# A hybrid trunk layer: low weight parts kept in DRAM for a second use, low slices issued last, pools waiting by bytes

## The chip, the cores and the metric

The kernel runs on one core of one Trainium2 chip. A core has five engines that run their own instruction streams: TensorE (PE, matmuls, with its weight loads shown as PEld), VectorE (DVE), ScalarE (ACT), GpSimd (POOL) and SyncE (SP, which here only issues DMAs). The metric is the time of one execution on the device in microseconds (us). A profile is one such execution, recorded instruction by instruction.

## What is computed

One layer of a streaming encoder trunk on 1024 prompt tokens and 32 sample tokens, width 1024, all in fp32. Three mixers share one input projection, a merge and a layer norm follow, and then PEER, a layer of single-neuron experts: 8 heads, each choosing 16 of 128 x 128 experts by product keys.

```python
z = x @ w_in + b_in                      # 12 sections of 1024 columns
y_a = (a_b * conv3(a_c * a_x)) @ w_out_a
y_b = (gelu(b_g) * rg_lru(conv4(b_x) + conv_b_b)) @ w_out_b
y_c = (rmsnorm(hgrn2(silu(c_q), 1 - f, c_i, log(f))) * silu(c_g)) @ w_out_c
merged = sigmoid(g_a) * y_a + sigmoid(g_b) * y_b + sigmoid(g_c) * y_c
x = layer_norm(ALPHA * x + merged @ w_o)
x = layer_norm(ALPHA * x + peer(x))

def peer_block(xt, wq, keys, u_tab, v_tab):
    q = (xt @ wq).reshape(n, 8, 2, 128)
    s = einsum('nhpd,hpkd->nhpk', q, keys)
    sv, si = top_k(s, 16)                       # per half
    top_s, top_p = top_k(sv[:, :, 0, :, None] + sv[:, :, 1, None, :], 16)
    expert = cid[top_p]                         # si0 * 128 + si1
    g = softmax(top_s)
    h = gelu(einsum('nd,nhkd->nhk', xt, u_tab[expert]))
    return einsum('nhk,nhkd->nd', g * h, v_tab[expert])
```

## The kernel before

**Tiling.** Activations lie transposed, 128 channels by tokens. Tokens are worked in two blocks: b=0 with 512 prompt tokens, b=1 with the other 512, a gap of 3 and the 32 sample tokens (548 columns, cut in two pieces of 274). Projections work on weight tiles of 128 input channels x 8 slices x 128 output channels (512 KB).

**Projections in split precision.** `weight` (L286) makes one weight tile ready: SP loads the raw fp32 tile into `wraw` (L300), ACT rounds it to the high part `wh` (L292), DVE subtracts, which leaves the low part `wl` (L293). All three have two buffers in the pool `wp` (topk1 keeps eight in `wk`). Activations are split the same way into `h`/`l` pairs (`dh`/`dl` in the dense stage). `proj` (L319) runs over the 8 slices and issues for each, and for each piece of tokens, wh by high (L326) and wh by low (L327), and then wl by high (L329), all into one PSUM tile `z`.

**Stages.** `first` works block 0: the heads of mixer C with mixer A between them, the three output projections, `norm1` (w_o), and then the two halves of its top-k (topk0.0, topk0.1, 256 tokens each, weights wq), between which mixer A of block 1 is put. `last` works block 1: heads with output A and gates, outputs C and B, norm1 in two parts, topk1 in two parts. The layer's experts come by two ways:

- For block 0 `gather` fetches them: for each of four tiles of 128 tokens, 128 rows-per-token of u and 128 of v, each an indirect DMA of 512 KB issued by POOL (L1210) into one of four `row` buffers. DVE multiplies and sums a u row (L1219, with a read of the accumulator) and multiplies and adds a v row (L1227). These 1024 DMAs and 1024 DVE instructions run beside everything else from the end of topk0.0 on; how many stand beside each stage is given by the seven numbers of `BESIDE`, counted against PE's instructions between marks (`cuts`).
- For block 1 the dense stage computes all 16,384 experts. 40 hidden tiles are made ahead, one-hot weights are spread to DRAM (`gd`, L1072/1073), and then 16 times: 8 projections of `ut`, 8 of `vt` over 544 tokens, accumulated by DVE into `acc` (L1141).

**Which weights are used more than once.** w_in's 96 tiles twice (block 0 and 1), w_out_b's and w_out_c's 8 twice, w_o's 8 three times, wq's 16 in topk0.0, again in topk0.1, and 24 times in topk1. w_out_a goes in plain fp32 in block 1 (`proj32`). `ut` and `vt` (256 tiles) are used once.

**What orders the work.** A scheduler that simulates the program puts the instructions of every engine in an order when the kernel is built; each engine then runs its own in that order, and waits on semaphores. SP's DMAs are issued in order too, so one that waits holds those behind it. Pools of tiles are opened and closed by stage (`open`, L117); a pool opened over bytes of a closed one waits for the closed one to be done with.

The changed functions and what calls them:

Of the kernel before, what the change touches and what calls it, by code (L numbers as in the profile page):

```python
# [10 lines left out]
F32 = mybir.dt.float32  # L11
# [11 lines left out]
KT = 8  # L23
# [54 lines left out]
class Lay:  # L78


    def __init__(self, n, cut=None, o=0):
        self.N, self.o = n, o
        cut = cut or (n if n <= 512 else n // 2)
        self.segs = [(o, cut)] + ([(o + cut, n - cut)] if cut < n else [])
# [17 lines left out]
class K:  # L102
    def __init__(self, ctx, tc, io):
        self.ctx, self.tc, self.nc, self.io = ctx, tc, tc.nc, io
        pool = lambda name, bufs, **k: ctx.enter_context(tc.tile_pool(name=name, bufs=bufs, **k))
        self.cst = pool("cst", 1)
        self.xp = pool("xp", 8)
        self.wp = pool("wp", 2)
        self.bp = pool("bp", 1)
        self.gp = pool("gp", 1)  # L110
        self.dp = pool("dp", 1, space=bass.MemoryType.DRAM)
        self.wpool, self.nraw = (self.wp, 2), 0
        self.rawp = [self.wpool]
        self.fetched = {}
        self.xs, self.ms = ([], []), ([None] * 8, [None] * 8)
        self.consts()

    def open(self, ctx, **pools):

        for name, (bufs, kw) in pools.items():  # L120
            setattr(self, name, ctx.enter_context(self.tc.tile_pool(name=name, bufs=bufs, **kw)))

    def et(self, n=556, dt=F32):
        return self.ep.tile([128, n], dt, name="e", tag="e")
# [158 lines left out]
        V.memset(self.st, 0.0)  # L283


    def weight(self, ap):  # L286
        nc = self.nc
        raw = self.weight32(ap)
        pool, bufs = self.wpool
        wh = pool.tile([128, KT, 128], F32R, name="wh", tag="wh", bufs=bufs)  # L290
        wl = pool.tile([128, KT, 128], F32R, name="wl", tag="wl", bufs=bufs)
        nc.scalar.copy(wh, raw)  # L292
        nc.vector.tensor_sub(wl, raw, wh.bitcast(F32))  # L293
        return wh, wl

    def weight32(self, ap):
# [4 lines left out]
        return raw  # L301

    def win(self, sec, ct):
        return self.fetched.pop((sec, ct), None) or self.weight(self.io["w_in"][sec * 8 + ct])

    def split(self, t, n, pool):
        nc = self.nc
# [11 lines left out]
    def proj(self, w, x, lay):  # L319
        mm = self.nc.tensor.matmul  # L320
        z = self.zz(lay)
        wh, wl = w
        for k in range(KT):
            xh, xl = x[k]
            for (o, n), ps in zip(lay.segs, z):
                mm(ps[:, :n], wh[:, k, :], xh[:, o:o + n], start=k == 0, stop=False)  # L326
                mm(ps[:, :n], wh[:, k, :], xl[:, o:o + n], start=False, stop=False)  # L327
            for (o, n), ps in zip(lay.segs, z):
                mm(ps[:, :n], wl[:, k, :], xh[:, o:o + n], start=False, stop=k == KT - 1)  # L329
        return z  # L330
# [6 lines left out]
                                      start=k == 0, stop=k == KT - 1)  # L337
        return z

    def outp(self, ap, y, lay):  # L340
        if isinstance(y[0], tuple):
            return self.proj(self.weight(ap), y, lay)
        return self.proj32(self.weight32(ap), y, lay)

    def at(self, b):
# [46 lines left out]
    def first(self, pick):  # L392

        nc, b = self.nc, 0
        with ExitStack() as c:
            self.open(c, yq=(8, {}))
            self.ypool = None, self.yp
            self.at(0)
            self.fetched = {(C_F, 0): self.win(C_F, 0)}
            self.load(0)  # L400
            MARK(nc, "mix_ca0")
            y = []
            oraw = self.heads(lambda h: y.append(self.mix_a(h)))
            cm = c.enter_context(ExitStack())
            self.open(cm, mp=(8, {}))
            MARK(nc, "out_a0")
            for d in range(8):
                self.out_piece(d, "w_out_a", G_A, y)
                if d == RMS:
                    rs = self.rms(oraw)  # L410
            y, gs = self.outs(oraw, rs)
            MARK(nc, "out_b0")
            for d in range(8):
                self.join(d, "w_out_b", y, gs[d], L0)
            self.load(1)
            m = [self.yfin(t) for t in self.m]
            cm.close()
            with ExitStack() as c2:
                self.open(c2, np_=(2, {}))
                MARK(nc, "norm0")  # L420
                lng = self.lnvec("ln1_g", self.np_, 1), self.lnvec("ln1_b", self.np_, 1)
                xT = self.norm1(m, self.tiles(0), L0, lng, lambda: self.pair(self.yq, "yh", "yl"))
            self.open(c, rp=(12, {}))
            self.ypool = self.yp, None
            self.at(0)
            ya = []
            for i, part in enumerate((Lay(256), Lay(256, o=256))):
                self.at(1)
                MARK(nc, f"mix_a1.{i}")
                ya.append(self.mix_a(len(ya)))  # L430
                self.at(0)
                MARK(nc, f"topk0.{i}")
                unit, end = self.topk(self.tiles(0)[2 * i:2 * i + 2], part, xT)
                for hg in range(4):
                    unit(hg, lambda j: self.weight(self.io["wq"][hg * 4 + j]), self.keys(hg, self.ep))
                for f in end():
                    self.at(1)
                    pick(f)
                    if not self.cuts:
                        self.cuts.append(len(nc.cur_bb.bb.instructions))  # L440
                    ya.append(self.mix_a(len(ya)))
            return ya

    def last(self, ya, cy, cs):
        nc = self.nc
# [5 lines left out]
        with ExitStack() as c:  # L451
# [21 lines left out]
            y, _ = self.outs(oraw, self.rms(oraw), zg)  # L473
# [3 lines left out]
            with ExitStack() as c2:  # L477
# [8 lines left out]
                y = [self.halves(t, self.et(dt=F32R), over(self.y2, "y") if k else self.et(dt=F32R))  # L486
                     for k, t in enumerate(y)]
                m = []
# [9 lines left out]
        with ExitStack() as c:  # L498
            self.open(c, wk=(1, {}))
            MARK(nc, "topk1")  # L500
            parts = [self.topk(of(flat), flat, xT) for _, flat in PARTS]
            held = {}
            for i, hg in ORDER:
                if hg not in held:
                    keys = self.keys(hg, self.wk)
                    self.wpool = (self.wk, 8) if hg > 1 else (self.wp, 2)
                    f = lambda j, hg=hg: self.weight(self.io["wq"][hg * 4 + j])
                    ws = []
                    if hg > 1:
                        held[hg] = lambda j, ws=ws, f=f: ws[j] if j < len(ws) else ws.append(f(j)) or ws[j], keys  # L510
                parts[i][0](hg, *held.get(hg, (f, keys)))
            self.wpool = self.wp, 2
            return xT, [s for _, end in parts for s in end()]
# [322 lines left out]

    def join(self, d, wname, y, g, L):
        nc, V = self.nc, self.nc.vector
        py = self.outp(self.io[wname][d], y, L)
        new = self.m[d] is None  # L840
        m = self.m[d] = self.mp.tile([128, NG], F32, name="m", tag="m") if new else self.m[d]
        for v, p in L.each(py):
            V.scalar_tensor_tensor(v(m if new else g), v(g), 1.0, p, op0=OP.add, op1=OP.mult)
        if not new:
            c = slice(L.o, L.o + L.N)
            V.tensor_add(m[:, c], m[:, c], g[:, c])
# [28 lines left out]
    def norm1(self, m, tiles, lay, lng, x1):  # L875
        nc = self.nc
# [1 line left out]
        rT = []  # L878
        w = 556 // N
        for d in range(8):  # L880
            ps = self.outp(self.io["w_o"][d], m, lay)
            if d % w == 0:
                t = self.et()
            rT.append(t[:, d % w * N:(d % w + 1) * N])
            A.copy(rT[d], ps[0][:, :N])
        xT = [x1() for _ in range(KT)]
        for ti, g0, o, n in tiles:
# [11 lines left out]
            for half in range(2):  # L899
                pt = self.tt()  # L900
                for j in range(4):
                    k = half * 4 + j
                    nc.tensor.transpose(pt[:, j * 128:j * 128 + n], xt[:n, k * 128:(k + 1) * 128],
                                        self.ident[:n, :n])
                for j in range(4):
                    xh, xl = xT[half * 4 + j]
# [488 lines left out]
```

## Time and profile before

| | us |
| --- | --- |
| runs (3) | 4188.08, 4206.25, 4211.31 |
| median | 4206.25 |
| the profiled execution | 4205.61 |
| its span in the profile | 4203.8 |
| mean granted TensorE clock | 0.952 |
| PE busy | 3815.1 |
| DVE busy | 3389.8 |
| POOL busy | 1591.6 |
| ACT busy | 1461.2 |
| moved by DMA | 973.51 MB, mean 232 GB/s |

Busy times are those of instructions of one profiled execution. A group's row in the profile names line, engine, operation, the tile written and those read with their shapes, then the count, the busy time in us, the mean of one in ns, the idle time just before them and what ended most of it. A row of the waits gives the waiting engine, tile and line, what it waited for, then us in total, times, and the longest. The granted clock is a share of full speed.

### The profile page before, as it was taken

The page shows a single profiled execution, that of the slowest core. Times are in us where ns is not written, and L with a number is a line of the kernel's source. Part 1 is how long each engine was busy: PE and PEld are TensorE (multiplying, and loading weights), DVE is VectorE, ACT ScalarE, POOL GpSimd, SP SyncE. Part 2 cuts the span into 40 slices and gives each one's busy share as a digit, 9 for nine tenths or more (in the row PEclk, how much of TensorE's full clock was granted, in tenths as well). Part 3 has the DMA queues.
Part 4 walks back from the last instruction along what each step waited for, and adds up shares of the span by engine and source line. Part 5 has one row for each costly group of instructions (what it writes and reads, how often), then busy time and mean ns, then how long its engine had stood idle before and what let it go on. Part 6 is the DMA issues. An engine that isn't in the chain of part 4 may idle for free.

```text
span 4203.8 us, 69644 instructions
## 1 busy us (share of the span) xinstructions
PE 3815.1 (91%) x26917; PEld 3564.2 (85%) x26917; DVE 3389.8 (81%) x6793; ACT 1461.2 (35%) x2358; POOL 1591.6 (38%) x1353
## 2 busy tenths in 40 slices
PE   9999999998866998998878999789999999999997
PEld 7888777787765896998868999689999999999997
DVE  6565448589997787998899999967788878777888
ACT  3333337332212222454233389822222222222222
POOL 0000000002453344444552478823355555455553
PEclk9999999999887998999989999899999999999998
DMA  3222222345785666778986888698889988888886
GB/s 109 76 71 78 90 92 92 129 154 195 255 284 183 197 226 194 249 271 279 316 287 206 266 247 245 202 325 302 283 315 325 324 303 312 299 313 302 311 313 243
DMA packets 333451, 973.51 MB, mean 232 GB/s; under 512 B 29952, under 2 KB 104832, under 8 KB 331072
## 3 DMA queue, kind: packets, MB, share of 16 engines
q0 software_dynamic: 147456, 536.94, 37.6%
q1 hardware_dynamic: 185664, 432.12, 30.3%
q8 instruction: 212, 3.47, 0.3%
q14 instruction: 119, 0.97, 0.1%
HBM read 912.40 MB, written 56.54 MB: 230 GB/s over the span
## 4 chain that ended last, share of the span: by engine, by line
PE 50%; DVE 15%; issue 14%; DMA 10%; POOL 9%; ACT 2%; POOLq 0%; SPq 0%; DVEq 0%; ACTq 0%
PE z L329 14%; PE z L326 14%; PE z L327 14%; POOL row L1210 9%; DMA row<-in_v,ex 6%; DVE row L1219 2%; DVE wl L293 2%; DVE x1g L1227 2%; DMA row<-in_u,ex 2%; PE t L1073 2%; PE t L681 1%; PE z L336 1%; DVE oa L1069 1%; DVE e L960 1%; DVE e L959 1%
## 5 line engine op out<-in xcount | busy, mean ns | idle before, releaser
L326 PE MATMUL z<-h,wh 128*128 128x272 f32 (+5 forms) x4608 | 1381.8, 313 | 104.6 <-ACT xe L637 59.8
L327 PE MATMUL z<-l,wh 128*128 128x272 f32 (+5 forms) x4608 | 1377.5, 311 | 6.0 <-DVE l L908 4.8
L292 ACT CAST wh<-wraw 128x1024 fp32r<-128x1024 f32 x568 | 595.5, 1049 | 1850.5 <-PE z L327 1538.4
L1210 POOL DMA_INDIRECT row<-in_u,ex x512 | 669.0, 1307 | 1432.6 <-DVE ex L1033 667.5
L329 PE MATMUL z<-h,wl 128*128 128x272 f32 (+5 forms) x4608 | 1172.7, 312 | 10.2 <-DVE wl L293 10.1
L326 PEld LDWEIGHTS z<-h,wh 128*128 128x128 f32 x4608 | 883.0, 192 | 152.0 <-ACT xe L637 60.1
L1210 POOL DMA_INDIRECT row<-in_v,ex x512 | 682.9, 1334 | 797.5 <-DVE x1g L1227 532.2
L327 PEld LDWEIGHTS z<-l,wh 128*128 128x128 f32 x4608 | 883.4, 192 | 42.3 <-DVE l L908 5.9
L293 DVE TENSOR_TENSOR wl<-wraw,wh 128x1024 fp32r<-128x1024 f32 x568 | 692.4, 1220 | 232.5 <-ACT wh L292 231.2
L329 PEld LDWEIGHTS z<-h,wl 128*128 128x128 f32 x4608 | 778.3, 191 | 50.0 <-DVE wl L293 14.0
L1227 DVE SCALAR_TENSOR_TENSOR x1g<-row,hh,x1g 128x1024 f32<-128x1024 f32 x512 | 655.3, 1280 | 105.1 <-DMA row<-in_v,ex 101.6
L1219 DVE SCALAR_TENSOR_TENSOR row<-row,x1g 128x1024 f32<-128x1024 f32 x512 | 619.3, 1221 | 98.8 <-DMA row<-in_u,ex 98.0
L326 PE MATMUL z<-dh,wh 128*128 128x272 f32 x2048 | 556.2, 293 | 9.3 <-ACT ge L1084 4.9
L327 PE MATMUL z<-dl,wh 128*128 128x272 f32 x2048 | 558.2, 294 | 1.1 <-DVE dl L1128 1.1
L329 PE MATMUL z<-dh,wl 128*128 128x272 f32 x2048 | 436.0, 295 | 74.6 <-DVE wl L293 74.4
L326 PEld LDWEIGHTS z<-dh,wh 128*128 128x128 f32 x2048 | 391.5, 194 | 12.3 <-ACT ge L1084 5.2
L329 PEld LDWEIGHTS z<-dh,wl 128*128 128x128 f32 x2048 | 331.2, 194 | 79.4 <-DVE wl L293 79.4
L327 PEld LDWEIGHTS z<-dl,wh 128*128 128x128 f32 x2048 | 391.7, 193 | 1.7 <-DVE dl L1128 1.5
L1072 POOL TENSOR_SCALAR ob<-iota,tr 128x128 f32<-128x128 f32 x272 | 218.6, 818 | 29.4 <-PE t L1073 13.0
L329 PE MATMUL z<-yh,wl 128*128 128x512 f32 (+1 forms) x512 | 179.4, 353 | 22.5 <-DVE wl L293 22.4
L1127 ACT CAST dh<-w 128x544 fp32r<-128x544 f32 x128 | 82.5, 648 | 335.8 <-DVE w L1123 335.4
L1073 PE MATMUL t<-ob,oa 128*128 128x128 f32 x1088 | 172.8, 295 | 25.1 <-DVE oa L1069 8.5
(382 smaller groups left out, 4828.3 us busy)
## 6 DMA issues: line engine op xcount, KB each, us to landing
wraw<-in_w_in SPq DMA_DIRECT2D x192, 512.0 KB, 3.5
wraw<-in_vt SPq DMA_DIRECT2D x128, 512.0 KB, 6.4
wraw<-in_ut SPq DMA_DIRECT2D x128, 512.0 KB, 5.6
gd<-stg SPq DMA_DIRECT2D x34, 1024.0 KB, 6.1
gt<-gd SPq DMA_DIRECT2D x16, 2176.0 KB, 10.7
wraw<-in_wq SPq DMA_DIRECT2D x56, 512.0 KB, 4.3
wraw<-in_w_o SPq DMA_DIRECT2D x24, 512.0 KB, 4.9
hd<-ge SPq DMA_DIRECT2D x40, 272.0 KB, 4.8
```

The lines of the kernel that those rows point to most:

```text
L292: nc.scalar.copy(wh, raw)
L293: nc.vector.tensor_sub(wl, raw, wh.bitcast(F32))
L326: mm(ps[:, :n], wh[:, k, :], xh[:, o:o + n], start=k == 0, stop=False)
L327: mm(ps[:, :n], wh[:, k, :], xl[:, o:o + n], start=False, stop=False)
L329: mm(ps[:, :n], wl[:, k, :], xh[:, o:o + n], start=False, stop=k == KT - 1)
L336: self.nc.tensor.matmul(ps[:, :n], w[:, k, :], x[k][:, o:o + n], start=k == 0, stop=k == KT - 1)
L1072: G.tensor_scalar(ob, self.iota, tr[:, 1, t:t + 1], None, op0=OP.is_equal)
L1073: nc.tensor.matmul(pw[:, s * 128:(s + 1) * 128], oa, ob, start=True, stop=True)
L1127: A.copy(hi, w)
L1210: nc.gpsimd.indirect_dma_start(out=u[:n], out_offset=None, in_=self.io[tab], in_offset=bass.IndirectOffsetOnAxis(ap=ex[:n, s:s + 1], axis=0))
L1219: V.scalar_tensor_tensor(u[:n], u[:n], 1.0, x1[:n], op0=OP.mult, op1=OP.mult, accum_out=hh[:n, s:s + 1])
L1227: V.scalar_tensor_tensor(x1[:n], u[:n], hh[:n, s:s + 1], x1[:n], op0=OP.mult, op1=OP.add)
```

## The change

1. `weight` takes a key. At a key's first use the low part is computed as before and is also stored to a DRAM tile of its own (SP, new L301). At later uses SP loads it from there into `wl` (new L295), and DVE does no subtraction. Keys are given for w_in, w_out_b, w_out_c, w_o and wq: 136 stores and 168 loads of 512 KB.
2. `proj` issues all slices' high-weight matmuls first, and then all slices' low-weight matmuls (new L339).
3. `open` asks for pools that wait for the tiles whose bytes they take over, instead of for the whole closed pool.
4. `outp` takes the weight's name and index, which makes the key.

Line numbers move: the cast L292 to L293, the subtraction L293 to L297, raw loads L300 to L308, matmuls L326, L327, L329 to L334, L335, L339, the rows' DVE instructions L1219 and L1227 to L1230 and L1238, `ex` L1033 to L1044.

```diff
--- before.py
+++ after.py
@@ -111,14 +111,15 @@
         self.dp = pool("dp", 1, space=bass.MemoryType.DRAM)
         self.wpool, self.nraw = (self.wp, 2), 0
         self.rawp = [self.wpool]
-        self.fetched = {}
+        self.fetched, self.low = {}, {}
         self.xs, self.ms = ([], []), ([None] * 8, [None] * 8)
         self.consts()
 
     def open(self, ctx, **pools):
 
         for name, (bufs, kw) in pools.items():
-            setattr(self, name, ctx.enter_context(self.tc.tile_pool(name=name, bufs=bufs, **kw)))
+            setattr(self, name, ctx.enter_context(self.tc.tile_pool(
+                name=name, bufs=bufs, reuse_waits="tile", **kw)))
 
     def et(self, n=556, dt=F32):
         return self.ep.tile([128, n], dt, name="e", tag="e")
@@ -283,14 +284,21 @@
         V.memset(self.st, 0.0)
 
 
-    def weight(self, ap):
+    def weight(self, ap, key=None):
         nc = self.nc
         raw = self.weight32(ap)
         pool, bufs = self.wpool
         wh = pool.tile([128, KT, 128], F32R, name="wh", tag="wh", bufs=bufs)
         wl = pool.tile([128, KT, 128], F32R, name="wl", tag="wl", bufs=bufs)
         nc.scalar.copy(wh, raw)
+        if key in self.low:
+            nc.sync.dma_start(wl.bitcast(F32), self.low[key])
+            return wh, wl
         nc.vector.tensor_sub(wl, raw, wh.bitcast(F32))
+        if key:
+
+            self.low[key] = self.dp.tile([128, KT, 128], F32, name="wl%d" % len(self.low))
+            nc.sync.dma_start(self.low[key], wl.bitcast(F32))
         return wh, wl
 
     def weight32(self, ap):
@@ -301,7 +309,7 @@
         return raw
 
     def win(self, sec, ct):
-        return self.fetched.pop((sec, ct), None) or self.weight(self.io["w_in"][sec * 8 + ct])
+        return self.fetched.pop((sec, ct), None) or self.weight(self.io["w_in"][sec * 8 + ct], ("w_in", sec * 8 + ct))
 
     def split(self, t, n, pool):
         nc = self.nc
@@ -325,6 +333,8 @@
             for (o, n), ps in zip(lay.segs, z):
                 mm(ps[:, :n], wh[:, k, :], xh[:, o:o + n], start=k == 0, stop=False)
                 mm(ps[:, :n], wh[:, k, :], xl[:, o:o + n], start=False, stop=False)
+        for k in range(KT):
+            xh, _ = x[k]
             for (o, n), ps in zip(lay.segs, z):
                 mm(ps[:, :n], wl[:, k, :], xh[:, o:o + n], start=False, stop=k == KT - 1)
         return z
@@ -337,9 +347,10 @@
                                       start=k == 0, stop=k == KT - 1)
         return z
 
-    def outp(self, ap, y, lay):
+    def outp(self, name, d, y, lay):
+        ap = self.io[name][d]
         if isinstance(y[0], tuple):
-            return self.proj(self.weight(ap), y, lay)
+            return self.proj(self.weight(ap, name != "w_out_a" and (name, d)), y, lay)
         return self.proj32(self.weight32(ap), y, lay)
 
     def at(self, b):
@@ -432,7 +443,7 @@
                 MARK(nc, f"topk0.{i}")
                 unit, end = self.topk(self.tiles(0)[2 * i:2 * i + 2], part, xT)
                 for hg in range(4):
-                    unit(hg, lambda j: self.weight(self.io["wq"][hg * 4 + j]), self.keys(hg, self.ep))
+                    unit(hg, lambda j: self.weight(self.io["wq"][hg * 4 + j], ("wq", hg * 4 + j)), self.keys(hg, self.ep))
                 for f in end():
                     self.at(1)
                     pick(f)
@@ -504,7 +515,7 @@
                 if hg not in held:
                     keys = self.keys(hg, self.wk)
                     self.wpool = (self.wk, 8) if hg > 1 else (self.wp, 2)
-                    f = lambda j, hg=hg: self.weight(self.io["wq"][hg * 4 + j])
+                    f = lambda j, hg=hg: self.weight(self.io["wq"][hg * 4 + j], ("wq", hg * 4 + j))
                     ws = []
                     if hg > 1:
                         held[hg] = lambda j, ws=ws, f=f: ws[j] if j < len(ws) else ws.append(f(j)) or ws[j], keys
@@ -836,7 +847,7 @@
 
     def join(self, d, wname, y, g, L):
         nc, V = self.nc, self.nc.vector
-        py = self.outp(self.io[wname][d], y, L)
+        py = self.outp(wname, d, y, L)
         new = self.m[d] is None
         m = self.m[d] = self.mp.tile([128, NG], F32, name="m", tag="m") if new else self.m[d]
         for v, p in L.each(py):
@@ -878,7 +889,7 @@
         rT = []
         w = 556 // N
         for d in range(8):
-            ps = self.outp(self.io["w_o"][d], m, lay)
+            ps = self.outp("w_o", d, m, lay)
             if d % w == 0:
                 t = self.et()
             rT.append(t[:, d % w * N:(d % w + 1) * N])
```

The orders below list an engine's instructions with the numbers that the build gives to tiles; `wl0` to `wl135` are the new DRAM tiles.

SP near the start of the kernel, before, in the first use of w_in:

```order
L300 DMA wraw_361<-in_w_in 128x1024
L517 DMA keys_6744<-in_keys 128x512
L300 DMA wraw_394<-in_w_in 128x1024
L300 DMA wraw_427<-in_w_in 128x1024
L300 DMA wraw_464<-in_w_in 128x1024
```

and now:

```order
L308 DMA wraw_363<-in_w_in 128x1024
L528 DMA keys_6984<-in_keys 128x512
L301 DMA wl0_276<-wl_273 128x1024
L308 DMA wraw_398<-in_w_in 128x1024
L301 DMA wl1_369<-wl_366 128x1024
L308 DMA wraw_433<-in_w_in 128x1024
```

A store now stands between each two raw loads. SP at the start of block 1's heads, in the second use, before:

```order
L300 DMA wraw_10047<-in_w_in 128x1024
L300 DMA wraw_10107<-in_w_in 128x1024
L300 DMA wraw_10167<-in_w_in 128x1024
L300 DMA wraw_10231<-in_w_in 128x1024
L300 DMA wraw_10291<-in_w_in 128x1024
```

and now:

```order
L308 DMA wraw_10379<-in_w_in 128x1024
L295 DMA wl_10187<-wl47_3211 128x1024
L308 DMA wraw_10439<-in_w_in 128x1024
L295 DMA wl_10258<-wl0_276 128x1024
L308 DMA wraw_10503<-in_w_in 128x1024
L295 DMA wl_10322<-wl1_369 128x1024
```

Each low load follows the raw load of the weight two further on. DVE at the end of topk0, where block 0's last expert indices `ex` are made, before:

```order
L1219 SCALAR_TENSOR_TENSOR row_39394,hh_39061<-row_39394,x1g_39062 128x1024
L1027 TENSOR_REDUCE r_9364<-r_9398 128x8x8
L1017 TENSOR_TENSOR r_9378<-r_9377 128x128
L1024 TENSOR_TENSOR r_9402<-r_9378,io16_87 128x512
L1024 TENSOR_TENSOR r_9406<-r_9378,io16_87 128x1024
L1026 TENSOR_TENSOR r_9402<-r_9402,r_9312 128x512
L1026 TENSOR_TENSOR r_9406<-r_9406,r_9312 128x1024
L1027 TENSOR_REDUCE r_9364<-r_9402 128x8x8
L1027 TENSOR_REDUCE r_9364<-r_9406 128x8x8
L1033 SCALAR_TENSOR_TENSOR ex_9410<-r_9364 128x128
```

and now:

```order
L1230 SCALAR_TENSOR_TENSOR row_39531,hh_39333<-row_39531,x1g_39334 128x1024
L1035 TENSOR_TENSOR r_9674<-r_9650,io16_87 128x512
L1035 TENSOR_TENSOR r_9678<-r_9650,io16_87 128x1024
L1037 TENSOR_TENSOR r_9674<-r_9674,r_9584 128x512
L1230 SCALAR_TENSOR_TENSOR row_39534,hh_39333<-row_39534,x1g_39334 128x1024
L1037 TENSOR_TENSOR r_9678<-r_9678,r_9584 128x1024
L1038 TENSOR_REDUCE r_9636<-r_9674 128x8x8
L1230 SCALAR_TENSOR_TENSOR row_39537,hh_39333<-row_39537,x1g_39334 128x1024
L1038 TENSOR_REDUCE r_9636<-r_9678 128x8x8
L1230 SCALAR_TENSOR_TENSOR row_39540,hh_39333<-row_39540,x1g_39334 128x1024
L1044 SCALAR_TENSOR_TENSOR ex_9682<-r_9636 128x128
```

Row tiles are numbered in threes from row_39064 before and row_39336 now, so row_39394 was the 111th row and row_39540 is the 69th: fewer rows stand ahead of `ex`, more behind it. PE at the start of the dense stage, before:

```order
L326 MATMUL z_25466<-dh_25400,wh_25462 128x272
L327 MATMUL z_25466<-dl_25401,wh_25462 128x272
L326 MATMUL z_25467<-dh_25400,wh_25462 128x272
L327 MATMUL z_25467<-dl_25401,wh_25462 128x272
L329 MATMUL z_25466<-dh_25400,wl_25463 128x272
L329 MATMUL z_25467<-dh_25400,wl_25463 128x272
```

and now, around the border between the high and the low slices of that projection:

```order
L335 MATMUL z_25796<-dl_25721,wh_25792 128x272
L335 MATMUL z_25797<-dl_25721,wh_25792 128x272
L334 MATMUL z_25796<-dh_25728,wh_25792 128x272
L334 MATMUL z_25797<-dh_25728,wh_25792 128x272
L335 MATMUL z_25738<-dl_25729,wh_25734 128x272
L335 MATMUL z_25739<-dl_25729,wh_25734 128x272
L339 MATMUL z_25738<-dh_25672,wl_25735 128x272
L339 MATMUL z_25739<-dh_25672,wl_25735 128x272
```

The first matmul on the low part moves from the fifth of a projection's 48 matmuls to the 33rd, and here the scheduler has put high slices of the next projection (`z_25796`, `wh_25792`) ahead of it as well.

## The prediction

> **What bounds the kernel now.** I read the page's totals and groups, then a table of stretches between VectorE (DVE) landmarks (first top-k MAX8, last expert-index `ex`, last `sb` step, last scan, last residual split of norm1, last top-k of block 1, first `acc` add), then waits, chain and DMA of each stretch. The stretches' rows give length, then busy time with count for PE, its weight loads, DVE, ACT and POOL, the granted clock, DMA share and GB/s.
>
> ```profile
> span 4203.8 us, 69644 instructions
> PE 3815.1 (91%) x26917; PEld 3564.2 (85%) x26917; DVE 3389.8 (81%) x6793; ACT 1461.2 (35%) x2358; POOL 1591.6 (38%) x1353
> L293 DVE TENSOR_TENSOR wl<-wraw,wh 128x1024 fp32r<-128x1024 f32 x568 | 692.4, 1220 | 232.5 <-ACT wh L292 231.2
> L1227 DVE SCALAR_TENSOR_TENSOR x1g<-row,hh,x1g 128x1024 f32<-128x1024 f32 x512 | 655.3, 1280 | 105.1 <-DMA row<-in_v,ex 101.6
> L1219 DVE SCALAR_TENSOR_TENSOR row<-row,x1g 128x1024 f32<-128x1024 f32 x512 | 619.3, 1221 | 98.8 <-DMA row<-in_u,ex 98.0
> ...
> core 0: us, PE busy (x) PEld busy (x) DVE busy (x) ACT busy (x) POOL busy (x), PEclk, DMA share, GB/s
> 0.00:896.00 896.00, 878.16 (x4589) 713.79 (x4590) 527.67 (x946) 341.46 (x457) 10.42 (x25) 1.00 0.29 97
> 896.00:1292.00 396.00, 289.83 (x2123) 279.51 (x2121) 384.04 (x1284) 89.63 (x138) 147.79 (x118) 0.89 0.69 232
> 1292.00:1659.00 367.00, 340.51 (x2675) 306.77 (x2675) 288.86 (x525) 95.81 (x193) 141.74 (x130) 0.93 0.60 195
> 1659.00:1957.00 298.00, 280.82 (x2037) 272.48 (x2038) 281.33 (x407) 142.19 (x212) 133.98 (x100) 0.96 0.77 259
> 1957.00:2210.00 253.00, 198.03 (x1380) 188.63 (x1378) 216.88 (x337) 73.41 (x135) 133.97 (x96) 0.87 0.87 301
> 2210.00:2659.00 449.00, 414.64 (x3222) 407.44 (x3223) 445.38 (x1517) 277.54 (x534) 258.88 (x278) 0.96 0.76 236
> 2823.00:4152.00 1329.00, 1250.11 (x9734) 1242.86 (x9734) 1072.48 (x1424) 338.02 (x498) 671.13 (x500) 0.97 0.88 310
> ```
>
> TensorE (PE) is 91% busy over the span, but not everywhere: 896 to 1292 is DVE's (384 of 396 us, PE 290); the next two are near PE's; 1957 to 2210 fills no engine but has DMA at 301 GB/s; 2210 to 2659 is DVE's again (445 of 449); dense is PE's with 79 us idle. The profiled execution took 4205.6 us, span 4203.8; it lies 0.6 under the runs' median of 4206.25, so the sum is made against 4205.6. The runs spread from 4188.08 to 4211.31: about 0.5%, 21 us, is what can be told from no change.
>
> **Subtractions replaced by loads.** 136 weights are stored (96 w_in, 8 w_out_b, 8 w_out_c, 8 w_o, 16 wq) and 168 loaded (96, 8, 8, 16, 40); 168 x 1.22 = 205 us of DVE work go, and 304 SP DMAs of 0.524 MB come. What that is worth depends on where the work stood. Counting the two orders between the landmarks, for subtractions and gather rows (a row is 1.22 + 0.08 for u, 1.28 for v, here 1.30 and 1.28): 896–1292: 54 to 9, 111 to 69; 1292–1659: 26 to 0, 102 to 143; 1659–1957: 38 to 0, 100 to 88; 1957–2210: 40 to 0, 96 to 82; 2210–2659: 55 to 41, 76 to 102; dense unchanged (206, 509). So rows as well as subtractions leave the first DVE stretch, and are paid later.
>
> *0 to 896*: stores only, at 97 GB/s and with PE at 878 of 896. SP has each store behind a raw load and ahead of the next; that next raw load already waited for the same subtraction to free `wraw`, so the new store wait holds it no longer: 0.
>
> *896 to 1292*: DVE loses 45 x 1.22 + 42 x 1.30 = 110, leaving 274. PE, 290, is next, and DMA:
>
> ```profile
> by line: DVE row L1219 22.5%; DVE wl L293 11.1%; DMA row<-in_u,ex 9.1%; issue 6.4%; PE z L329 4.9%; PE z L326 4.9%; PE z L327 4.8%; DVE e L960 3.4%; DVE e L959 3.4%; DVE e L962 3.0%; DVE e L958 2.7%; DVE e L961 2.5%; DVE r L1024 2.2%; DVE r
> DMA packets 25617, 91.70 MB, mean 232 GB/s; under 512 B 2848, under 2 KB 2848, under 8 KB 25586
> 4100.00:4150.00 50.00, 50.00 (x402) 50.00 (x401) 42.78 (x47) 15.15 (x24) 26.79 (x20) 1.00 0.96 347
> ```
>
> Bytes: 91.7 - 42 rows x 0.524 + 45 loads + 16 stores = 101.7 MB. The chain there is led by row and wl work on DVE, so the time falls to the next limit: 101.7 MB at dense's 310 GB/s is 328 us, at the busiest 50 us in the trace (347) 293. I take 328, the rate held over 1329 us: -68; bounds -103 and -40 (if row latency, 9% of the chain, grows).
>
> The Trainium skill's "DMA: Bandwidth & Descriptors", § Measured, has 425 GB/s for one core alone (16 MB transfers). No row here comes to it: the best 50 us show 347. By 425 this stretch would be PE's (-106) and 1957–2210 would give 37, in all an estimate of 4034; the measured row decides.
>
> *Pools by bytes.* In this stretch PE stands still once:
>
> ```profile
> PE z L326 <- ACT xe L637: 59.8, 2, 59.5
> 1291.95 0.84 ACT L647 ACTIVATE xe<-e,f,f 128x544 f32<-128x544 f32 x1 [33.46 <-DVE ex L1033]
> ```
>
> ACT's first `xe` write waits for the closed pool's last DVE instruction, `ex`, and PE behind ACT for 59.5 us. Now it waits for a reduction 14 DVE instructions earlier, six of them rows: 6 x 1.3 + small ones, about 11 us. I count 0 beside the -68, since DVE and DMA must still do the stretch's work (bounds -11 and 0). At the other pool borders the last owner of the bytes is the same work.
>
> *1292 to 1659*: +41 rows x 1.28 - 26 x 1.22 = +21 on DVE, which rises to 310. Its row waits also grow:
>
> ```profile
> DVE x1g L1227 <- DMA row<-in_v,ex: 18.5, 12, 4.0
> DVE row L1219 <- DMA row<-in_u,ex: 10.2, 5, 3.4
> ```
>
> 28.7 for 102 rows becomes 40 for 143. DVE 310 + 40 = 350 against a PE that needs 341 of 367: half shows, +15 (bounds 0 and 33).
>
> *1659 to 1957*: DVE loses 61, but PE needs 281 of 298: -10 (0 to -17).
>
> *1957 to 2210*: DVE loses 66.
>
> ```profile
> by line: issue 28.2%; POOL row L1210 23.2%; DMA row<-in_u,ex 7.4%; DMA row<-in_v,ex 6.3%; DMA wraw<-in_w_in 6.1%; DVE wl L293 3.4%; PE z L329 3.2%; PE z L327 3.1%; DVE x1g L1227 3.0%; DVE row L1219 2.9%; PE z L326 2.9%; DMA wraw<-in_wq 2.4%
> DMA packets 21151, 76.07 MB, mean 301 GB/s; under 512 B 2506, under 2 KB 2506, under 8 KB 21133
> wraw<-in_w_o SPq DMA_DIRECT2D x16, 512.0 KB, 5.4
> wraw<-in_wq SPq DMA_DIRECT2D x12, 512.0 KB, 5.8
> ```
>
> The chain is rows: issue, POOL, landing. Per row 253 / 96 = 2.64 us, so 82 rows would take 216 (-37). But 40 loads for 14 rows less make 89.7 MB, 289 us at 310 (+36). I take 0, the middle.
>
> *2210 to 2659*: DVE has no slack; +26 x 1.28 - 14 x 1.22 = +16 (0 to 16).
>
> **Low slices last, in dense.** No subtraction goes here, but wl is needed 28 of a projection's 48 matmuls later.
>
> ```profile
> PE z L329 <- DVE wl L293: 76.1, 22, 9.2
> DVE x1g L1227 <- DMA row<-in_v,ex: 75.5, 50, 7.0
> DVE row L1219 <- DMA row<-in_u,ex: 59.3, 39, 5.5
> ...
> 3406.25 1.28 DVE L1227 SCALAR_TENSOR_TENSOR x1g<-row,hh,x1g 128x1024 f32<-128x1024 f32 x1 [5.30 <-DMA row<-in_v,ex]
> 3407.80 1.26 DVE L293 TENSOR_TENSOR wl<-wraw,wh 128x1024 fp32r<-128x1024 f32 x1
> 3409.11 0.82 PE L329 MATMUL z<-dh,wl 128*128 128x272 f32 x2 [9.23 <-DVE wl L293]
> ...
> 3409.00:3414.00 5.00, 4.89 (x21) 4.89 (x22) 4.37 (x6) 0.00 (x0) 1.64 (x1) 0.50 0.88 304
> 3414.00:3463.00 49.00, 49.00 (x392) 49.00 (x391) 38.91 (x42) 10.21 (x13) 26.93 (x21) 1.00 0.80 279
> ```
>
> 22 stalls, each a subtraction queued on DVE behind a row that had not landed (here 5.3 us late). The last row gives a matmul 49 / 392 = 0.125 us, so wl gains 28 x 0.125 = 3.5 us; PE also pays after a stall: 21 matmuls in 5 us at clock 0.50 where 40 would fit, 2.4 us. In the trace eight of the stalls, 53 us together, are longer than 3.5 and would each keep the rest: 8 x 3.5 = 28 goes; the other fourteen go wholly, 76 - 53 = 23. With stalls that go or shrink to little goes PE's slow start; I count five such, 12. That is -63. What is late next is the row itself, and a dense stage of 1266 us would carry its 412 MB at 326 GB/s instead of 310, which makes rows later still, and with them the subtractions: I take -50 (bounds -63 and 0).
>
> **Sum**: -68 + 15 - 10 + 0 + 16 - 50 = -97; 4205.6 - 97 = **4109 us**, in runs too.
>
> **The loads' own wait.** Where wl(i) is loaded, the load stands on SP behind raw(i+2), waits until PE has finished projection i-2, and holds the raw loads behind it. From that release to the first low slice PE has projection i-1 and the high slices of i: (48 + 32) x 0.125 = 10 us for 544 tokens, and (24 + 16) x 0.118 = 4.7 us for 256 tokens (topk0.1, norm1, topk1: 48 of the loads), 0.118 being 0.125 x 256 / 272. Loads landed in 5.4 to 5.8 us between 1957 and 2210, so the 256-token ones come up to 1 us late there; 28 of the 48 lie in that stretch, 28 us, inside its bound of +36.
>
> **The rivals.**
> Slower: these 48 loads decide. If a load lands 8 us after issue (below, 10.5 for the larger `gt` and 11.4 for two raw loads at the end of a stretch show that landings stretch so far), each comes 3 us late, PE waits 48 x 3 = 144 and the time is 4109 + 144 = 4253. It pays back the whole gain from 4.7 + 97 / 48 = 6.7 us on. Against: 5.8 now; for: bytes there rise 18%. Chance 0.12.
>
> ```profile
> gt<-gd SPq DMA_DIRECT2D x13, 2176.0 KB, 10.5
> wraw<-in_w_out_b SPq DMA_DIRECT2D x2, 512.0 KB, 11.4
> ```
>
> No change: PE is 91% busy, and DVE time freed at one place is taken by the rows moved. The first stretch falls only 40, 1292 to 1659 and 2210 to 2659 take back the whole +21 and +16, and dense keeps its stalls because its rows stay late: 4205.6 - 3 = 4203. For it: rows end on DMA, which the change loads further; against: DVE's 384 of 396, with 106 us of room before PE. Chance 0.13. The Trainium skill's "Perfetto Trace Analysis", § Identifying the Most-Contended Engine, would improve the most occupied engine first; by it, with PE leading over the span, this change gives little. The stretch's row differs from the whole span's.
>
> Less: dense stalls stay, the rest comes: 4109 + 50 = 4159; row waits of 135 us in dense speak for it. Chance 0.15.
>
> More: DVE was the limit through three stretches and DMA follows at 347 GB/s or better: -103, 0, -17, -37, 0 and -63 make -220 at most, 3986; halfway from the sum to it, 4047. For: DVE 81% in the mean. Chance 0.15.
>
> The likeliest, 4109 within 4075 to 4140, has 0.45. The range leaves out the slower rival and the far half of the gain: 4020 to 4200. Faster by over 0.5% (under 4185): 0.45 + 0.15 + 0.15 = 0.75; within: 0.13; slower: 0.12.
>
> **What would show it.** The subtraction group at x400 and 168 loads; the first DVE stretch under 340 us; PE's idle before `xe` under 50; PE's wait for wl in dense near 25; rows per us unchanged in 1957–2210. I am wrong if PE's waits for loaded wl exceed 50 us, if DVE's row waits swallow the freed time, or if dense keeps 60 us of wl waits.

## The result and the profile after

The changed kernel takes 4102.06 us (median of 4 runs, 4098.35 to 4103.25) against 4202.66 for the kernel before beside it: a ratio of 0.9763, 95% interval 0.9733 to 0.9792. The forecast was 4109, which is 97 us under the profiled 4205.6; the medians here lie 100.6 apart. Its profile's span is 4096.2 us, 107.6 under the one before; the time is looked for in these two traces. The execution profiled after is the fastest of its four.

First lines of the kernel after: totals, two groups, and the DMA row that is new.

```profile
span 4096.2 us, 69951 instructions
PE 3799.3 (93%) x26917; PEld 3543.6 (87%) x26917; DVE 3205.3 (78%) x6625; ACT 1471.7 (36%) x2352; POOL 1528.8 (37%) x1353
L297 DVE TENSOR_TENSOR wl<-wraw,wh 128x1024 fp32r<-128x1024 f32 x400 | 488.5, 1222 | 187.4 <-ACT wh L293 89.7
L339 PE MATMUL z<-h,wl 128*128 128x272 f32 (+5 forms) x4608 | 744.6, 309 | 14.9 <-DMA wl<-wl 14.2
wl<-wl SPq DMA_DIRECT2D x304, 512.0 KB, 4.7
```

The subtractions are 400 instead of 568, 204 us less, and 304 new DMAs stand for them (136 stores and 168 loads). Then the same stretches between the same DVE landmarks, after:

```profile
core 0: us, PE busy (x) PEld busy (x) DVE busy (x) ACT busy (x) POOL busy (x), PEclk, DMA share, GB/s
0.00:886.00 886.00, 869.51 (x4542) 706.92 (x4543) 520.43 (x941) 340.46 (x450) 10.41 (x25) 1.00 0.50 173
886.00:1185.00 299.00, 272.45 (x2099) 264.38 (x2098) 283.05 (x1151) 91.92 (x139) 76.69 (x75) 0.99 0.89 324
1185.00:1571.00 386.00, 358.28 (x2748) 320.80 (x2746) 306.62 (x589) 98.32 (x195) 190.42 (x173) 0.92 0.82 287
1571.00:1843.00 272.00, 264.46 (x1971) 257.36 (x1972) 225.71 (x339) 145.11 (x213) 107.50 (x87) 0.99 0.90 324
1843.00:2101.00 258.00, 201.63 (x1399) 192.07 (x1398) 158.21 (x292) 68.77 (x128) 93.08 (x82) 0.86 0.92 348
2101.00:2574.00 473.00, 423.32 (x3254) 412.59 (x3255) 463.30 (x1530) 282.74 (x535) 287.60 (x303) 0.95 0.83 275
2574.00:2743.00 169.00, 139.36 (x967) 128.44 (x967) 130.45 (x285) 93.25 (x180) 88.31 (x105) 0.94 0.82 268
2743.00:4048.00 1305.00, 1252.71 (x9807) 1243.78 (x9806) 1077.21 (x1433) 339.88 (x498) 671.08 (x502) 0.99 0.90 316
4048.00:4096.00 48.00, 17.58 (x143) 17.26 (x141) 40.32 (x73) 11.26 (x18) 3.74 (x3) 0.71 0.38 130
```

Two more rows of the kernel before, for the stretches that the prediction's table leaves out:

```profile
2659.00:2823.00 164.00, 138.63 (x970) 128.71 (x970) 127.51 (x278) 90.77 (x176) 87.61 (x102) 0.94 0.82 271
4152.00:4204.00 52.00, 24.35 (x200) 23.97 (x198) 45.69 (x81) 12.33 (x19) 6.07 (x6) 0.76 0.41 137
```

A landmark can move against PE's work, so a stretch's length alone misleads: the first stretch is 10 us shorter with 47 matmuls less in it, which now run in a later one. Length minus PE busy, PE's idle time, suffers less from it:

| stretch before | its length before, after | forecast | PE idle before, after |
| --- | --- | --- | --- |
| 0–896 | 896, 886 | 0 | 18, 16 |
| 896–1292 | 396, 299 | -68 | 106, 27 |
| 1292–1659 | 367, 386 | +15 | 26, 28 |
| 1659–1957 | 298, 272 | -10 | 17, 8 |
| 1957–2210 | 253, 258 | 0 | 55, 56 |
| 2210–2659 | 449, 473 | +16 | 34, 50 |
| 2659–2823 | 164, 169 | 0 | 25, 30 |
| dense, and its last 50 us | 1381, 1353 | -50 | 107, 83 |

PE idles 389 us before and 297 after: -92. The other 16 of the 108 are PE's own busy time, 3815 to 3799 at a granted clock of 0.952 and then 0.967. The waits of PE in dense, after:

```profile
DVE x1g L1238 <- DMA row<-in_v,ex: 87.0, 68, 6.1
DVE row L1230 <- DMA row<-in_u,ex: 69.6, 52, 6.9
PE z L339 <- DVE wl L297: 23.8, 7, 4.4
PE z L335 <- DVE dl L1139: 21.0, 17, 2.7
PE z L334 <- ACT dh L1138: 6.8, 11, 1.7
```

The wait for low parts falls from 76.1 us in 22 waits to 23.8 in 7. Two waits are new, for `dl` and `dh`, 28 us together: PE has none for them in the kernel before. DVE's waits for rows rise from 135 to 157.

### The profile page after: what moved, and what is told of

Same layout as the page of the kernel before. It is cut to its first block, busy times and chain, and to the rows that moved or that the text cites. A ratio compares the mean times of both kernels' runs of the same rounds, so it can differ in the third digit from the quotient of the medians.

```text
span 4096.2 us, 69951 instructions
## 1 busy us (share of the span) xinstructions
PE 3799.3 (93%) x26917; PEld 3543.6 (87%) x26917; DVE 3205.3 (78%) x6625; ACT 1471.7 (36%) x2352; POOL 1528.8 (37%) x1353
## 4 chain that ended last, share of the span: by engine, by line
PE 16%; DMA 11%; issue 9%; DVE 7%; POOL 6%; ACT 2%; SPq 0%; POOLq 0%; DVEq 0%; ACTq 0%
DMA row<-in_v,ex 7%; POOL row L1221 6%; PE z L339 5%; PE z L335 5%; PE z L334 4%; DVE x1g L1238 2%; PE t L1084 1%; DMA row<-in_u,ex 1%; DVE oa L1080 1%; DMA wl<-wl 1%; DVE wl L297 1%; ACT stg L1085 1%; DMA wraw<-in_wq 1%; DMA ge<-hd 1%; ACT ob L1074 0%
## 5 line engine op out<-in xcount | busy, mean ns | idle before, releaser
L334 PE MATMUL z<-h,wh 128*128 128x272 f32 (+5 forms) x4608 | 1315.4, 313 | 30.4 <-ACT wh L293 18.0
L335 PE MATMUL z<-l,wh 128*128 128x272 f32 (+5 forms) x4608 | 1303.7, 310 | 1.2 <-DVE l L370 1.2
L1221 POOL DMA_INDIRECT row<-in_u,ex x512 | 628.0, 1227 | 1510.0 <-DVE ex L1044 655.8
L293 ACT CAST wh<-wraw 128x1024 fp32r<-128x1024 f32 x568 | 596.3, 1050 | 1414.1 <-PE z L335 1130.7
L334 PEld LDWEIGHTS z<-h,wh 128*128 128x128 f32 x4608 | 878.0, 191 | 77.1 <-ACT wh L293 21.5
L335 PEld LDWEIGHTS z<-l,wh 128*128 128x128 f32 x4608 | 878.8, 191 | 37.4 <-issue 2.7
L339 PE MATMUL z<-h,wl 128*128 128x272 f32 (+5 forms) x4608 | 744.6, 309 | 14.9 <-DMA wl<-wl 14.2
L1238 DVE SCALAR_TENSOR_TENSOR x1g<-row,hh,x1g 128x1024 f32<-128x1024 f32 x512 | 655.1, 1280 | 125.4 <-DMA row<-in_v,ex 121.7
L1230 DVE SCALAR_TENSOR_TENSOR row<-row,x1g 128x1024 f32<-128x1024 f32 x512 | 618.2, 1217 | 145.0 <-DMA row<-in_u,ex 144.4
L339 PEld LDWEIGHTS z<-h,wl 128*128 128x128 f32 x4608 | 649.9, 190 | 49.6 <-DMA wl<-wl 15.5
L297 DVE TENSOR_TENSOR wl<-wraw,wh 128x1024 fp32r<-128x1024 f32 x400 | 488.5, 1222 | 187.4 <-ACT wh L293 89.7
L335 PE MATMUL z<-dl,wh 128*128 128x272 f32 x2048 | 518.1, 292 | 29.6 <-DVE dl L1139 29.4
L334 PE MATMUL z<-dh,wh 128*128 128x272 f32 x2048 | 515.3, 293 | 10.2 <-ACT dh L1138 9.8
L335 PEld LDWEIGHTS z<-dl,wh 128*128 128x128 f32 x2048 | 386.3, 192 | 35.1 <-DVE dl L1139 35.1
L334 PEld LDWEIGHTS z<-dh,wh 128*128 128x128 f32 x2048 | 384.6, 192 | 14.3 <-ACT dh L1138 14.2
L339 PE MATMUL z<-dh,wl 128*128 128x272 f32 x2048 | 283.9, 292 | 23.8 <-DVE wl L297 23.8
L339 PEld LDWEIGHTS z<-dh,wl 128*128 128x128 f32 x2048 | 269.8, 192 | 25.4 <-DVE wl L297 25.4
L1084 PEld LDWEIGHTS t<-ob,oa 128*128 128x128 f32 x1088 | 147.8, 199 | 47.5 <-POOL ob L1083 15.1
```

What stands on the lines that cost most here:

```text
L1084: nc.tensor.matmul(pw[:, s * 128:(s + 1) * 128], oa, ob, start=True, stop=True)
L1221: nc.gpsimd.indirect_dma_start(out=u[:n], out_offset=None, in_=self.io[tab], in_offset=bass.IndirectOffsetOnAxis(ap=ex[:n, s:s + 1], axis=0))
L1230: V.scalar_tensor_tensor(u[:n], u[:n], 1.0, x1[:n], op0=OP.mult, op1=OP.mult, accum_out=hh[:n, s:s + 1])
L1238: V.scalar_tensor_tensor(x1[:n], u[:n], hh[:n, s:s + 1], x1[:n], op0=OP.mult, op1=OP.add)
```

## The experiments

Each part alone first. All ratios are to the kernel before, run beside the experiment.

**The low slices last, alone.**

```diff
+        for k in range(KT):
+            xh, _ = x[k]
             for (o, n), ps in zip(lay.segs, z):
                 mm(ps[:, :n], wl[:, k, :], xh[:, o:o + n], ...
```

> The kernel before with the low slices last in every projection, and nothing else. My theory: this part earns the dense stage's share (28 us of the 107) and some of the 25 us of low-part waits between 896 and 1292, and leaves DVE's 168 subtractions where they were: 4155 to 4175 us, DVE still full between 896 and 1292, the 59 us pause of PE before xe still there. Rival (the slack alone hides the subtractions, the loads earn nothing): 4100 to 4120.

4167.81 us, ratio 0.9919 (0.9894 to 0.9944): 34 us. The pause before `xe` is there and longer, and the DVE-bound stretch remains (390 us from the first MAX8 to the last `ex`; dense and tail 1350, as in the changed kernel):

```profile
PE z L326 <- ACT xe L639: 73.9, 1, 73.9
ACT xe L649 <- DVE ex L1035: 45.5, 1, 45.5
PE z L327 <- DVE dl L1130: 18.2, 17, 2.7
PE z L326 <- ACT dh L1129: 8.6, 14, 1.2
```

The waits for `dl` and `dh` come with this part alone, too. The whole of dense's gain is this part's; the rival, that slack alone would hide the subtractions, is out.

**Pools that wait by bytes, alone.** `reuse_waits="tile"` in `open`, nothing else.

> The kernel before with pools that wait by bytes, and nothing else. My theory: PE's pause before xe shortens by about 11 us of its 59, since the reduction that xe then waits for stands only 14 DVE instructions ahead of ex: 4190 to 4203 us. Rival (the whole pause is the closed pool's): 4140 to 4150.

4193.84 us, ratio 0.9982 (0.9969 to 0.9995). The pause before `xe` keeps most of its length, and ACT waits for a reduction in place of `ex`:

```profile
PE z L327 <- ACT xe L638: 52.8, 2, 52.6
ACT xe L648 <- DVE r L1028: 26.1, 1, 26.1
```

59.5 became 52.6. The part is worth some 8 us while DVE is late.

**Stores and loads, alone.** The changed kernel with the old order of slices and the old pools.

> Stores and loads of low parts alone: low slices interleaved as before, pools wait for the whole closed pool. My theory: DVE is freed between 896 and 1292 (-70 to -95), dense gains nothing, and a loaded low part is needed after 2 or 4 matmuls instead of 16 or 32, so that PE waits some us for each load of a 256-token projection that lands 6 to 7 us after issue (48 of them, up to 4 us each): 4140 to 4260, PE's waits for loaded low parts over 80 us. Rival (loads are early in any order): 4125 to 4140, those waits under 40.

4130.27 us, ratio 0.9829 (0.9791 to 0.9868), the largest part, 72 us. The stretch to the last `ex` takes 306 us, with no pause before `xe` although pools wait as before; dense and tail take 1385, as before. My fear for the 256-token loads was wrong even without the slack:

```profile
PE z L336 <- DMA wl<-wl: 34.8, 25, 11.0
PE z L336 <- DVE wl L296: 90.5, 32, 9.2
```

PE waits 35 us for loaded low parts, not over 80, and the time lies in the rival's range. The longer wait, 90.5 us, is for low parts that DVE still computes.

**The changed kernel with the old pools.**

> The changed kernel with pools that wait for the whole closed pool, as before. My theory: with DVE's work cut, ex comes before xe is wanted or shortly after, so little comes back: 4100 to 4115 us. Rival (the pools' part removed the 59 us pause): 4150 to 4165.

4100.59 us, ratio 0.9753 (0.9723 to 0.9783), not to be told from 4102.06. No wait of `xe` for `ex` is left in its trace. So the pause of 59 us went because DVE came earlier, not because pools wait for less. The three parts alone give 34 + 8 + 72 = 114, together 100.6: the pools' 8 are contained in the loads' 72, and the other 5 lie inside the intervals.

Next, the gap in dense: forecast -50, measured -28.

**The first vt projection of each dense round in the old order.**

```diff
-                ps = self.proj(self.weight(io["vt"][jc, d]), ws, L)
+                ps = self.proj(self.weight(io["vt"][jc, d]), ws, L, d > 0)
```

`proj` has a new parameter here, `last`; where it is false (`d` = 0) the low slices stay between the high ones, as before.

> The changed kernel, but the first vt projection of each of the 16 dense rounds keeps the old order of slices. My theory: with all high slices first, PE needs the last dl of a round 15 matmuls sooner, and the 28 us of new waits for dl and dh in dense come from that; here they fall to 5 or less and the first projection's low part waits a little more: dense 15 to 25 us shorter, 4078 to 4092 us. Rival (dl is late because rows hold DVE, in any order): waits for dl stay above 15, 4095 to 4110.

4079.66 us, ratio 0.9709 (0.9687 to 0.9731), 22 us better than the changed kernel. Dense and tail take 1336 instead of 1353. Its waits in dense:

```profile
PE z L342 <- DVE wl L297: 16.3, 6, 4.7
PE z L334 <- ACT dh L1141: 9.8, 11, 2.3
PE z L335 <- DVE dl L1142: 7.6, 8, 2.2
PE z L338 <- DVE wl L297: 4.0, 4, 1.4
```

The wait for `dl` falls from 21.0 to 7.6, that for `dh` rises from 6.8 to 9.8, so the two keep 17 us where 5 were expected; PE's waits in dense fall from 52 to 38 us. For `dl` the cause is shown: with all high slices first, the last slice of a projection begins with the 29th of its 48 matmuls instead of the 43rd, so that a round's last `dl` is needed 14 matmuls sooner (the expectation says 15). That DVE makes it late because rows stand ahead is argued and not shown, and why PE still waits for `dh` stays open.

**Does DMA bound 1843 to 2101?** No stores and loads for w_out_b and w_o.

```diff
-            return self.proj(self.weight(ap, name != "w_out_a" and (name, d)), y, lay)
+            return self.proj(self.weight(ap, name == "w_out_c" and (name, d)), y, lay)
```

> The changed kernel without stores and loads for w_out_b and w_o: 16 stores and 24 loads fewer, 24 subtractions more on DVE, all between 1843 and 2101 us. My theory: that stretch is bound by DMA (89.7 MB at 348 GB/s, the highest rate of any stretch, DVE 158 of 258), so 12.6 MB less take up to 36 us off it, and DVE's 29 us more hide: 4070 to 4090 us. Rival A (row latency or DVE order bounds it): within 8 us of 4102. Rival B (DVE's subtractions are what delays there): 4110 to 4130.

4084.48 us, ratio 0.9722 (0.9703 to 0.9741); the interval overlaps the changed kernel's a little, the gain is some 18 us. It lies in the range of my theory, but by luck, since it isn't where I put it:

```profile
1840.40:2093.10 252.70, 196.75 (x1402) 190.03 (x1400) 189.66 (x329) 72.18 (x133) 108.19 (x86) 0.87 0.88 320
2093.10:2556.80 463.70, 419.95 (x3255) 410.68 (x3256) 456.89 (x1519) 280.88 (x532) 282.95 (x300) 0.95 0.83 272
```

The stretch moved 81 MB instead of 90 and went from 259 to 253 us, with the rate falling from 348 to 320 GB/s: were it bound by DMA, the rate would have stayed. 9 us more came off the stretch behind it. The theory that DMA limits the whole stretch fell; PE still idles 56 us, and what sets that stretch stays open.

**A second DMA beside each load.**

```diff
             nc.sync.dma_start(wl.bitcast(F32), self.low[key])
+            nc.sync.dma_start(self.dp.tile([128, KT, 128], F32, name="junk", tag="junk", bufs=8), self.low[key])
```

> The changed kernel with a second DMA beside each load of a low part, which copies the same 512 KB from DRAM to DRAM and is used by nobody: 88 MB more. My theory: two stretches stand at the DMA limit; at 347 GB/s the stretch from 1843 to 2101 gets 41 x 0.524 / 347 = 62 us longer, 886 to 1185 (47 loads, 122 MB) about 50, and the two between gain up to 40 together: 4200 to 4260 us. Rival (DMA still has room everywhere): 4100 to 4140.

4310.29 us, ratio 1.025 (1.0223 to 1.0278), outside both expectations, because the edit did not do what was meant. Nothing reads the copies, and 151 of the 168 came to lie in one stretch:

```profile
890.00:1420.00 530.00, 300.71 (x2103) 290.30 (x2102) 299.69 (x1176) 93.28 (x139) 91.62 (x86) 0.79 0.96 345
...
junk<-wl SPq DMA_DIRECT2D x151, 512.0 KB, 12.8
```

That stretch grew from 299 to 530 us, while the others kept their lengths within 22. It says nothing on them, but it shows what DMA carried when its engines were 96% busy: 345 GB/s over 530 us, with copies between DRAM tiles.

**Rows moved.** Two other paces of the gather, in the changed kernel: 20 rows earlier, or 20 later.

```diff
-BESIDE = 92, 125, 145, 94, 42, 82, 444
+BESIDE = 92, 125, 165, 84, 32, 82, 444
```

> The changed kernel with the gather's pace moved: 20 rows more beside heads1's outputs (145 to 165), 10 fewer beside norm1 and topk1 (94 to 84) and 10 fewer beside the spread (42 to 32). My theory: norm1's end to the last top-k search (2101 to 2574) is bound by DVE (463 of 473 us), and the dense gain was given back there; 20 rows less there are 20 x 1.28 = 26 us of DVE, of which 10 to 26 come off, and the stretch before it, with DVE 226 of 272, pays 0 to 10: 4075 to 4095 us. Rival (that stretch is PE's, 423 of 473, or the rows only move): 4098 to 4110.

4098.40 us, ratio 0.9749 (0.9728 to 0.977): not to be told from the changed kernel. 109 rows were still issued between norm1's end and the last top-k search (104 in the changed kernel), so this run moved no DVE time out of that stretch; it tells nothing of the theory.

```diff
-BESIDE = 92, 125, 145, 94, 42, 82, 444
+BESIDE = 92, 125, 145, 74, 42, 82, 464
```

> The changed kernel with 20 gather rows put off from norm1 and topk1 (94 to 74) to the dense stage (444 to 464); 19 rows fewer stand ahead of the last top-k search in DVE's order. My theory: the stretch from 2101 to 2574 is DVE's (463 of 473 us, 104 v rows), so 19 x 1.28 = 24 us less on DVE take 15 to 24 off it, and dense, which is PE's, pays 0 to 10: 4078 to 4097 us. Rival (PE or the top-k chain sets that stretch, rows only fill gaps): stretch within 8 us of 473, dense 0 to 10 longer, 4098 to 4112.

4093.66 us, ratio 0.9729 (0.9704 to 0.9754): 8 us better by the medians and 14 by the ratios, with intervals that overlap. Here the rows did leave (84 issued):

```profile
2100.80:2549.60 448.80, 418.72 (x3267) 412.07 (x3268) 438.30 (x1512) 283.29 (x536) 263.76 (x286) 0.96 0.80 266
2711.50:4091.90 1380.40, 1274.39 (x9947) 1266.24 (x9945) 1144.31 (x1535) 351.98 (x518) 707.31 (x525) 0.96 0.88 311
```

The stretch is 24 us shorter, as DVE's 25 us less would have it, and PE's idle time in it goes from 49 to 30. Dense and tail, with the same 9947 matmuls, take 1380 instead of 1353: PE idles 106 instead of 83. So both theories were half right: rows on DVE do set the stretch, and dense has no free place for 20 more; by this trace they cost there what they had cost before.

**The two edits that helped, together.** The first vt projections in the old order, and no loads for w_out_b and w_o.

> The changed kernel with both edits that helped: the first vt projection of each dense round in the old order of slices, and no stores and loads for w_out_b and w_o. They work in different stretches, so if each has the cause that I give, their gains of 22 and 18 us add: 4055 to 4070 us. Rival (both only free the same later wait): 4075 to 4085.

4071.54 us, ratio 0.9668 (0.9642 to 0.9693), clearly better than the changed kernel and 1.5 us above the range. By the ratios the gains add (0.0054 and 0.0041 apart, 0.0095 together); by the medians 22 and 18 come to 31 together, which the intervals can't tell from 40. It is the best version found. Put off rows do nothing for it:

> e12_both with 20 gather rows put off from norm1 and topk1 to dense as in e11_defer. My theory after e11_defer: the rows' time leaves the stretch to the last top-k search, but the hidden-tile matmuls that ran there come after it, so that PE gains only what idle it loses, 8 us at most: 4060 to 4074 us, about even with e12_both (4071.5). Rival (dense has PE room for the rows now that its dl waits are gone, and the 16 us of PE idle come off in full): 4050 to 4058.

4073.81 us, ratio 0.9688 (0.9669 to 0.9707), even with it, as expected after the run before.

## Why the prediction was right, point by point

**The sum.** -97 was forecast; the medians gave -100.6 and the traces -107.6. So near a hit is in part luck. By PE's idle time the first DVE stretch gave 12 us more than forecast (80 for 68), 1292 to 1659 cost 14 less, dense gave 26 less (24 for 50), and 16 us came off PE's own busy time, which I hadn't counted; these nearly cancel.

**The signs.** Four of the five came: x400 and 168 loads, 299 us in the first DVE stretch, no pause before `xe`, 23.8 us of waits for `wl` in dense. The fifth did not: the rows issued from 1957 to 2210 fell from 96 in 253 us to 82 in 258.

**896 to 1292, forecast -68, measured -97.** The first half of the mechanism held: DVE's busy time fell by 101 (forecast 110), and PE's idle time with it, 106 to 27. What was mis-sized is the next limit. I let DMA hold the stretch with 101.7 MB at 310 GB/s, the mean of dense.

```profile
DMA packets 27057, 96.98 MB, mean 324 GB/s; under 512 B 2995, under 2 KB 2995, under 8 KB 27028
```

The missing bytes are 15 us at my rate, the higher rate the other 14; and since the run with the copies moved 345 GB/s in this stretch, though with another mix of transfers, 324 need not have been a limit. DVE is still the fullest engine here, busy 283 of 299 us (95%, 97% before). The stretch shrank by about what DVE lost, so DVE may lead it still; no run tests that. For a short time DMA had more to give than the trace before shows; these are the busiest 40 us, before and then after:

```profile
2760.00:2800.00 40.00, 39.62 (x316) 39.39 (x315) 30.96 (x37) 7.80 (x9) 12.29 (x10) 1.00 0.97 360
1850.00:1890.00 40.00, 32.04 (x223) 31.49 (x222) 21.48 (x35) 8.50 (x13) 15.07 (x16) 0.83 1.03 407
```

A DMA share above 1 says that such a row is good to a few per cent only. The Trainium skill's "DMA: Bandwidth & Descriptors", § Measured, with 425 GB/s for one core alone, is nearer to these 40 us than my 347. The estimate from it fits the first DVE stretch (-106 for -97) no better than my bound from 347 (-103), and it erred for 1957 to 2210, which was to give 37 and gave nothing.

**1957 to 2210, forecast 0.** PE's idle time rose by 1, but the 0 was luck. It was the middle between a stretch paced by rows (-37) and one paced by bytes (+36). The bytes came as forecast, 89.7 MB, at 348 GB/s instead of 310; the rows per us fell; and with fewer loads the rate fell with the bytes. PE's largest wait there is now for loaded low parts, 19.6 of its 56 us; what sets the rest stays open.

**Pools by bytes, forecast 0 beside the loads.** Right: the kernel with the old pools is even, and the part alone gives 8 where the 11 us of earlier release would give at most 11.

**1292 to 1659, +15.** The stretch is 19 longer, but it holds 73 matmuls more, and PE's idle time rose by 1 only, so the 15 did not come as forecast: DVE's 307 us, with the moved rows, hid behind PE's 358. **1659 to 1957, -10.** PE's idle time fell by 10; the rest of its 26 is 66 matmuls fewer and a granted clock of 0.99 for 0.96. **2210 to 2659, +16.** PE's idle time rose by 15. Here the rows moved from the first stretch were paid, on the DVE-bound stretch that the forecast named.

**Dense, -50.** The low-part waits fell by 52 us, as forecast from the stalls' lengths (51; the eight long ones are 52 us together, not 53). The step that failed is "what is late next is the row itself": rows cost 22 us more of DVE's time, but that was DVE's; what PE came to wait for was `dl` and `dh`, 28 us that I hadn't counted though the same edit brings their need forward. So -28 for -50, and keeping the first vt projections in the old order got 17 of the 22 back.

**The rival with late loads.** The waits over the whole span, and the loads from 1843 to 2101 and then from 2101 to 2574 (the stores are over by 930 us):

```profile
PE z L339 <- DMA wl<-wl: 30.3, 17, 6.3
...
wl<-wl SPq DMA_DIRECT2D x41, 512.0 KB, 7.0
wl<-wl SPq DMA_DIRECT2D x14, 512.0 KB, 14.4
```

PE waited for loaded low parts 30.3 us in all, 19.6 of them in the first of these stretches, where 28 was my bound. The landing there was 7.0 us, past the 6.7 from which I had it eat the whole gain: that threshold was too harsh, since it charged each of the 48 loads with the delay, and PE waited 17 times for all 168. The 14 later loads landed in 14.4 us and PE waited 3 times, 4.8 us: the time to landing alone doesn't tell the wait.

**The rival that PE leads the span.** The Trainium skill's "Perfetto Trace Analysis", § Identifying the Most-Contended Engine, read over the span, pointed at PE (its weight loads 85% before, DVE 81%); its § Optimization Strategy says that the most contended engine can change over time between regimes, and the stretches show just that: DVE's stretch of 396 us gave 80 of the 92 us of PE idle that went.

## What to carry to other kernels

Cut the span at landmarks and ask in each piece which engine is full; work taken from an engine that leads in one stretch only is worth what it frees there, up to the next limit, and what is moved out of that stretch is paid again wherever the same engine leads a later one. Compare stretches by the idle time of the engine that carries the work, not by their length, since landmarks wander against the work. When an order of operands is changed to give one of them more time, ask which other operand is now needed sooner.

## What was not expected of the hardware

- DMA moved 407 GB/s over 40 us in the changed kernel and 411 over 44 us in the run with the copies (row below), where the busiest 40 us of the kernel before show 360; over 530 us with copies between DRAM tiles it held 345.

```profile
2064.00:2108.00 44.00, 36.70 (x261) 36.23 (x260) 23.00 (x38) 9.56 (x14) 15.97 (x17) 0.88 1.03 411
```

- Loaded low parts landed in 7.0 us (median) in a stretch where DMA was 92% busy, and PE waited for 6 of the 41, though for most of them the prediction had estimated 4.7 us from issue to first use.
